# Splitting gate and up weights by casting and adding DMAs in a two-layer decoder kernel

## The chip, the cores and the metric

The kernel runs on one core of one Trainium2 chip. The metric is the device time of one execution in microseconds; a smaller time is better. TensorE multiplies matrices, VectorE and GpSimd do elementwise work, ScalarE does functions and copies, SyncE only issues DMAs. Engines run independently and wait for each other by semaphores. In profiles they are called PE (PEld for its weight loads), DVE, POOL, ACT and SP.

## The reference

Two layers over 512 tokens of width 1024, all in float32. Each layer is a half-step feed-forward block (FFN), a mixer and another half-step FFN, every one between two RMS norms. The mixer of layer 0 is attention (stick-breaking and dilated heads), that of layer 1 an mLSTM in chunks. Only the FFN matters here; its hidden width is 2816, 22 tiles of 128:

```python
def _swiglu(x, w_gate, w_up, w_down):
    return (jax.nn.silu(x @ w_gate) * (x @ w_up)) @ w_down

hf = _swiglu(_rms_norm(x, g[0]), ffn_w_gate[layer, 0], ffn_w_up[layer, 0], ffn_w_down[layer, 0])
x = x + 0.5 * _rms_norm(hf, g[1])
```

The four FFNs run in the order: layer 0 before and after attention, layer 1 before and after the mLSTM. They are called the first to the fourth FFN.

## The kernel before, in words

TensorE reads operands of the type float32r, which keeps fewer bits than float32. To come near float32, each operand is kept as two float32r tiles, a high part (the value rounded) and a low part (value minus high part), and a product is three products: high by high, high by low, low by high (`mm3`, L169). All products are recorded at L72.

A chunk of weights is 128 x 1024 float32, 512 KB: for the projections, one tile of 128 hidden columns by all 1024 inputs. `chunk` (L120) loads it into a buffer `raw` (three buffers) with a DMA from SyncE's queue (L124), casts it on ScalarE into the high part `whi` (L127) and subtracts on VectorE, or on GpSimd where `eng` says so, into the low part `wlo` (L128). There are four buffers each for `whi` and `wlo`, so a chunk's parts can be written once TensorE is done with the chunk four before. `proj` (L175) takes one chunk: 8 tiles of the contraction by three products, 24 products of 128 x 512 for all tokens.

An FFN (`ffn`, L320) begins with the first tiles in two halves of the tokens, as their norm gets ready: two tiles (four chunks) in the first and third FFN, three tiles (six chunks, four of them in a pool of their own) in the second and fourth, which follow a mixer. These first chunks come from `first_chunks` (L143). From then on `up_to(f)` (L344) runs the gate and the up chunk of tile f, one after the other:

```python
                    for n in ("gate", "up"):
                        bs.append(self.bank("pg"))
                        self.proj(bs[-1], self.chunk(a[n][l, w, f]))
```

`glu` (L394) makes h from the two: silu on ScalarE (L396), times the row scales on GpSimd (L397), times the up projection on VectorE (L398). Sixteen of the 22 tiles go through the down projection in four groups of four, by a scheme with seven products instead of eight. `right` (L443) loads two tiles of the down weights, forms sums of their blocks on GpSimd (L451, L452, L455, L457) and splits them into `dhi` and `dlo` (`wop`, by `split`, L182: cast on ScalarE at L183, subtraction on VectorE at L184); `left` (L422) does the same for h (`hop`, `hhi` and `hlo`) with VectorE alone. The seven products of a group (`products`, L464, 12 matmuls into banks `pc` per product) are put between the four chunks of the next group's first two tiles, two behind each chunk, one behind the last. So in a group TensorE has four chunks with products between, and then four without. After the last group's products follow eight chunks without any, then the down projection of the last six tiles (banks `po`), with the norm and the start of the next phase.

The order on TensorE is the order in which the program emits matmuls. The other engines' instructions, DMA issues among them, are put in each engine's queue by a scheduler when the program is built: earlier statements have precedence, but one that isn't ready, by the scheduler's own reckoning, lets later ones pass. On the chip each queue then runs in that fixed order, and an instruction that waits holds all behind it.

Of the kernel before, what the change touches and what calls it, by code (L numbers as in the profile page):

```python
# [24 lines left out]
# key block -> (bank, first column, first column in a flat row of 1280)  # L25
BLK = {0: (0, 0, 0), 1: (1, 0, 512), 3: (1, 384, 896), 2: (2, 0, 1024)}
BANKS = ((0, 512), (512, 512), (1024, 256))
# groups of four tiles of the down projection by the scheme with seven products
# [4 lines left out]
# order of the main thread's work in the mixers, and waits (ns of the tensor engine's work)  # L33
# [9 lines left out]
class Trunk:  # L43
# [25 lines left out]
    # The tensor engine's work is emitted in the order in which it should run: the main  # L69
    # thread's products, with the steps of the waiting tasks put in where they get ready.  # L70
# [11 lines left out]
    def later(self, delay, d, key, value):  # L82
        """d[key] = value once the tensor engine has worked that long"""
        def task():
            d[key] = value
            return
            yield
        self.spawn(task(), delay)

    def step(self):  # L90
        """run the task that is ready first, up to its next wait"""
        self.tasks.sort(key=lambda t: t[:2])
        _, q, gen = self.tasks.pop(0)
        self.busy = True
        d = next(gen, None)
        self.busy = False
        if d is not None:
            self.tasks.append((self.clk + d, q, gen))
# [13 lines left out]
    def exp_ln(self):  # L112
        """load the table that has both Exp and Ln"""
        self.tc.keep_in_program_order(self.nc.scalar.preload_act_table_set("natural_log_exp_and_others"))

# [4 lines left out]
    def chunk(self, src, n=1024, pool=None, tag="w", bufs=4, eng=None):  # L120
        """a chunk of weights, split into two float32r parts"""
# [10 lines left out]

    def gates(self, src):
        """the weights of the gates: high and low parts side by side, for two passes"""
# [8 lines left out]
    def first_chunks(self, ph, between=None, pool=None):  # L143
        """the first four chunks of weights of a phase, one by one beside other work"""
# [30 lines left out]
    def proj(self, out, w, t0=0, t1=T):  # L175
        """out[:, t0:t1] = (chunk of weights, K tile after K tile)^T @ xn^T"""
# [17 lines left out]
    def gain_row(self, l, i):  # L194
        """the same for the first norm, with a small load, and copied to all partitions by a product with ones"""
# [10 lines left out]
    def rstd(self, src, f=1.0, eps=EPS, sums=None):  # L206
        """1 / root of (f x the mean square of 1024 columns + eps), in two steps of 512"""
# [16 lines left out]
    def row_scales(self, fp):  # L224
        """The scheme with seven products mixes tokens, so h of a token with a small xn would be lost beside
        that of others. As h goes with the square of xn, it is divided by q = mean square / (mean square + eps),
        with 1 / q rounded to bfloat16 and at most 1e16; the norm after the FFN takes the factor back by its eps.
        1 / q of all tokens, as rows on all partitions, and that eps."""
# [18 lines left out]
    def pre(self, tb, g, wait, to=None):  # L247
        """xn^T of 128 tokens, in two parts"""
# [19 lines left out]
    def half(self, h):  # L268
        """wait for xn^T of half of the tokens"""
# [4 lines left out]
    def chain(self, tb, g, gnext, ph, out):  # L274
        """x += norm(y) for 128 tokens, and the next norm"""
# [17 lines left out]
    def down(self, hs, ws, first, then=None):  # L293
        """y[tb] (+)= h[tb] @ w for a few tiles of the contraction; then(tb) after each"""
# [17 lines left out]
    # Down projection: for the first tiles of the contraction by the scheme of Strassen and Winograd  # L312
    # on 2 x 2 blocks (halves of the tokens, pairs of tiles of the contraction, halves of the columns),
    # with seven products instead of eight:
    #   S1 = A21 + A22   S2 = S1 - A11    S3 = A11 - A21   S4 = A12 - S2
    #   T1 = B12 - B11   T2 = B22 - T1    T3 = B22 - B12   T4 = B21 - T2
    #   1: A11 B11   2: A12 B21   3: S4 B22   4: A22 T4   5: S1 T1   6: S2 T2   7: S3 T3
    #   C11 = 1 + 2   C12 = 1 + 6 + 5 + 3   C21 = 1 + 6 + 7 + 4   C22 = 1 + 6 + 7 + 5
    # The sums of products gather in PSUM, and are added to y on the way.
    def ffn(self, l, w, then, prefetch):  # L320
        nc, a = self.nc, self.a
        tc = self.tc
        with tc.tile_pool(name=f"ffn{l}{w}", bufs=1, reuse_waits="tile") as fp:
# [16 lines left out]
            with tc.tile_pool(name=f"dn{l}{w}", bufs=1, reuse_waits="tile") as dp:  # L340
                self.fp, self.dp = fp, dp
                todo = []

                def up_to(f):  # L344
                    """projections up to tile f, with products of the down projection between them"""
# [3 lines left out]
                    for n in ("gate", "up"):  # L349
                        bs.append(self.bank("pg"))  # L350
                        self.proj(bs[-1], self.chunk(a[n][l, w, f]))
# [49 lines left out]
    def hop(self, src):  # L401
        """parts of 256 columns of h"""
# [4 lines left out]
    def wop(self, src):  # L407
        """parts of 512 columns of weights"""
# [13 lines left out]
    def left(self, o, e, d):  # L422
        """operands of the products from the tiles e and d of h; the last two on the call of the result"""
# [19 lines left out]
    def right(self, o, e, d):  # L443
        """the same from two tiles of the weights"""
# [19 lines left out]
    def products(self, A, B, rest, first):  # L464
        """the seven products, in an order in which no sum waits for its reading"""
# [35 lines left out]
    def out_part(self, ws, mix, po, tb, ks):  # L501
        """a part of the second half of the contraction of an output projection, for a block of tokens"""
# [10 lines left out]
    def out_first(self, src, mix, done):  # L513
        """of that half, for two blocks of tokens, the part that doesn't need the last heads"""
# [108 lines left out]
    def qk_split(self, pq, pk):  # L623
        """q (scaled by 1/8) and k of two heads in parts, for two passes instead of three: of head r,
# [516 lines left out]
```

## Time and profile before

| | |
|---|---|
| median of three runs | 2077.33 us (2076.93 to 2078.64) |
| profiled execution, span from first to last instruction | 2074.3 us |
| own time of the profiled execution | not listed apart from the span |
| busy TensorE, VectorE, ScalarE, GpSimd | 97%, 64%, 46%, 24% |
| moved by DMA | 200.51 MB, mean 97 GB/s |

A profile gives, for each engine, what it ran and when; idle time is put down to the instruction or DMA whose semaphore came last. A group of instructions is named by its line, engine, operation and tiles (out<-in). Matmuls are pipelined, so that one of them is listed with about 390 ns although the next begins after 0.23 us; the time of many is read from the chain or from stretches. The granted clock (PEclk) is TensorE's clock as a share of its full 2.4 GHz.

### The profile page before, as it was taken

What the parts mean: (1) busy time and instruction counts of PE and PEld (TensorE: products, weight loads), DVE (VectorE), ACT (ScalarE), POOL (GpSimd) and SP (SyncE); (2) the same over time, 40 slices, a digit from 0 to 9 for tenths busy, and PEclk for the clock granted to TensorE, in tenths of its full rate; (3) what the DMA queues carried; (4) which work ended last, traced back from release to release, by engine and by line L of the source; (5) the groups of instructions that cost most, each with busy time, mean ns of one, the idle gap of its engine ahead of it and who ended that gap; (6) DMA issues with size and microseconds to landing.
All of it is one profiled execution on the core that took longest, in us unless ns stands there. A gap on an engine that the chain in (4) does not pass through costs nothing. (4 is left out here: it accounts for less than half of the span.)

```text
span 2074.3 us, 25950 instructions
## 1 busy us (share of the span) xinstructions
PE 2018.6 (97%) x9876; PEld 1677.5 (81%) x9876; DVE 1320.4 (64%) x2016; ACT 948.3 (46%) x1633; POOL 503.9 (24%) x374
## 2 busy tenths in 40 slices
PE   8999999999998999999999999999999979999998
PEld 7888887788876878888888888888888869788887
DVE  6766654656567676665487666547776786766643
ACT  5443332466775353333344333324786554443321
POOL 4322302101002342320243223021010144332111
PEclk9999999999999999999999999999999999999999
DMA  5323232232122243333223333321433222423321
GB/s 183 122 93 109 94 112 81 81 108 67 57 63 70 72 132 102 102 102 112 61 91 123 94 108 94 112 76 43 146 97 127 89 91 92 130 94 104 109 82 41
DMA packets 56119, 200.51 MB, mean 97 GB/s; under 512 B 6521, under 2 KB 6649, under 8 KB 55994
## 3 DMA queue, kind: packets, MB, share of 16 engines
q1 hardware_dynamic: 55992, 198.85, 29.8%
q8 instruction: 77, 1.26, 0.3%
q14 instruction: 48, 0.39, 0.1%
q10 hardware_dynamic: 2, 0.00, 0.0%
HBM read 196.65 MB, written 4.80 MB: 97 GB/s over the span
## 5 line engine op out<-in xcount | busy, mean ns | idle before, releaser
L72 PE MATMUL pg<-xnl,whi 128*128 128x512 f32 (+1 forms) x1568 | 584.6, 373 | 6.2 <-DVE xnl L184 6.2
L72 PE MATMUL pg<-xnh,whi 128*128 128x512 f32 (+1 forms) x1568 | 584.7, 373 | 0.1
L72 PE MATMUL pg<-xnh,wlo 128*128 128x512 f32 (+1 forms) x1568 | 583.9, 372 | 0.0
L127 ACT CAST whi<-raw 128x1024 fp32r<-128x1024 f32 x248 | 259.4, 1049 | 455.6 <-issue 202.5
L128 DVE TENSOR_TENSOR wlo<-raw,whi 128x1024 fp32r<-128x1024 f32 x227 | 289.5, 1277 | 196.2 <-ACT whi L127 192.0
L72 PEld LDWEIGHTS pg<-xnl,whi 128*128 128x128 f32 x1568 | 297.5, 190 | 61.6 <-DVE xnl L184 7.0
L72 PEld LDWEIGHTS pg<-xnh,whi 128*128 128x128 f32 x1568 | 297.5, 190 | 55.2 <-ACT xnh L183 0.5
L72 PEld LDWEIGHTS pg<-xnh,wlo 128*128 128x128 f32 x1568 | 297.5, 190 | 54.8
L397 POOL TENSOR_TENSOR h<-h,rs 128x512 f32<-128x512 f32 x88 | 143.0, 1625 | 777.3 <-ACT h L396 749.5
L184 DVE TENSOR_TENSOR dlo<-raw,dhi 128x512 fp32r<-128x512 f32 x240 | 188.3, 804 | 92.6 <-ACT dhi L183 92.0
L183 ACT CAST dhi<-raw 128x512 fp32r<-128x512 f32 x240 | 146.5, 621 | 198.1 <-DMA raw<-down 153.2
L398 DVE TENSOR_TENSOR h<-h,pg 128x512 f32<-128x512 f32 x88 | 60.0, 682 | 224.8 <-PE pg L72 221.6
L72 PE MATMUL pc<-dhi,hhi 128*128 128x512 f32 x448 | 175.2, 391 | 3.9 <-ACT hhi L183 3.9
L72 PE MATMUL pc<-dhi,hlo 128*128 128x512 f32 x448 | 175.2, 391 | 0.6 <-DVE hlo L184 0.6
L72 PE MATMUL pc<-dlo,hhi 128*128 128x512 f32 x448 | 174.8, 390 | 0.0
L482 DVE TENSOR_TENSOR y<-y,pc 128x512 f32<-128x512 f32 x192 | 128.9, 677 | 5.6 <-PE pc L72 5.4
L72 PE MATMUL pq<-xnh,whi 128*128 128x512 f32 (+1 forms) x312 | 112.8, 363 | 0.0
L72 PE MATMUL pq<-xnl,whi 128*128 128x512 f32 (+1 forms) x312 | 112.0, 359 | 0.3 <-DVE xnl L184 0.3
L72 PE MATMUL pq<-xnh,wlo 128*128 128x512 f32 (+1 forms) x312 | 111.7, 358 | 0.0
L184 DVE TENSOR_TENSOR hlo<-h,hhi 128x256 fp32r<-128x256 f32 x208 | 103.3, 514 | 8.1 <-ACT hhi L183 7.9
L183 ACT CAST hhi<-h 128x256 fp32r<-128x256 f32 x208 | 78.9, 404 | 54.9 <-DVE h L398 47.7
L72 PEld LDWEIGHTS pc<-dhi,hhi 128*128 128x128 f32 x448 | 84.2, 188 | 22.5 <-ACT hhi L183 4.8
(236 smaller groups left out, 3323.2 us busy)
## 6 DMA issues: line engine op xcount, KB each, us to landing
raw<-gate SPq DMA_DIRECT2D x88, 512.0 KB, 3.5
raw<-up SPq DMA_DIRECT2D x88, 512.0 KB, 3.5
raw<-down SPq DMA_DIRECT2D x88, 512.0 KB, 3.5
raw<-mlstm_in SPq DMA_DIRECT2D x24, 512.0 KB, 3.5
raw<-attn_in SPq DMA_DIRECT2D x16, 512.0 KB, 3.5
bt<-rows SPq DMA_DIRECT2D x8, 896.0 KB, 4.5
gb<-norm_g SPq DMA_DIRECT2D x11, 512.0 KB, 3.9
raw<-attn_v SPq DMA_DIRECT2D x8, 512.0 KB
```

The costliest lines, as they stand in the source:

```text
L72: self.nc.tensor.matmul(out, lhsT=lhsT, rhs=rhs, start=start, stop=stop, skip_group_check=True)
L127: nc.scalar.copy(hi[:, :n], raw[:, :n])
L128: sub = (eng or nc.vector).tensor_sub(lo[:, :n], raw[:, :n], hi[:, :n])
L183: self.nc.scalar.copy(hi, src)
L184: self.nc.vector.tensor_sub(lo, src, hi)
L397: self.nc.gpsimd.tensor_mul(h, h, self.rs)
L398: self.nc.vector.tensor_mul(h, h, pu)
L482: self.nc.vector.tensor_add(dst, dst, b)
```

## The change

The loop of `up_to` no longer calls `chunk`. It takes its chunks from `stream`, a new function that issues both of a chunk's parts as DMAs from GpSimd's queue: a load of the float32 weights that casts into `whi`, a copy on ScalarE that writes the negative of `whi` into `wlo`, and a second load of the same weights that is added to what `wlo` holds. Casting loads are emitted up to two chunks ahead of the one in use, adding loads one ahead. The number of buffers stays, and so do `first_chunks`, the mixers and the down projection. All else in the diff takes out comments and docstrings.

```diff
+    def stream(self, srcs, tag="w", bufs=4):
+        nc, hs, ls = self.nc, [], []
+
+        def get(i):
+            while len(hs) < min(i + 3, len(srcs)):
+                hi = self.pp.tile([P, 1024], F32R, tag=tag + "hi", bufs=bufs, name="whi")
+                lo = self.pp.tile([P, 1024], F32R, tag=tag + "lo", bufs=bufs, name="wlo")
+                nc.gpsimd.dma_start(hi, srcs[len(hs)])
+                nc.scalar.activation(lo, hi.bitcast(F32), AF.Copy, scale=-1.0)
+                hs.append((hi, lo))
+            while len(ls) < min(i + 2, len(srcs)):
+                n = len(ls)
+                nc.gpsimd.dma_start(hs[n][1], srcs[n], accum_op=ALU.add)
+                ls.append(n)
+            return hs[i]
+        return get
...
+                f0 = len(hs)
+                get = self.stream([a[n][l, w, f] for f in range(f0, NF) for n in ("gate", "up")])
...
-                    for n in ("gate", "up"):
+                    for n in range(2):
                         bs.append(self.bank("pg"))
-                        self.proj(bs[-1], self.chunk(a[n][l, w, f]))
+                        self.proj(bs[-1], get(2 * (f - f0) + n))
```

## Rows read from the trace of the kernel before

**Rows 1.** The page, busy time by engine: us, share of the span, instructions.

```profile
span 2074.3 us, 25950 instructions
PE 2018.6 (97%) x9876; PEld 1677.5 (81%) x9876; DVE 1320.4 (64%) x2016; ACT 948.3 (46%) x1633; POOL 503.9 (24%) x374
```

**Rows 2.** Table of stretches: length, busy us by engine (count), PEclk, DMA share, GB/s.

```profile
60.00:343.00 283.00, 283.00 (x1227) 230.70 (x1226) 164.07 (x246) 106.68 (x180) 71.39 (x44) 1.00 0.33 106
...
1760.00:2030.00 270.00, 267.73 (x1159) 217.71 (x1158) 163.86 (x245) 101.88 (x177) 69.05 (x44) 1.00 0.32 100
...
1208.30:1271.96 63.66, 63.66 (x277) 51.94 (x277) 40.92 (x63) 23.75 (x40) 19.39 (x12) 1.00 0.32 99
```

**Rows 3.** Chain of waits, third FFN, merged: start us, us, what.

```profile
1072.26 36.55 PE pg L72 x192
...
1114.29 5.57 PE pg L72 x24
...
1271.96 27.88 PE pg L72 x120
...
1335.63 44.61 PE pg L72 x192
```

**Rows 4.** Groups of instructions by line: busy us, mean ns, idle before, releaser.

```profile
L128 DVE TENSOR_TENSOR wlo<-raw,whi 128x1024 fp32r<-128x1024 f32 x227 | 289.5, 1277 | 196.2 <-ACT whi L127 192.0
L127 ACT CAST whi<-raw 128x1024 fp32r<-128x1024 f32 x248 | 259.4, 1049 | 455.6 <-issue 202.5 <-PE pg L72 191.3 <-DMA raw<-up 23.2
...
L128 POOL TENSOR_TENSOR wlo<-raw,whi 128x1024 fp32r<-128x1024 f32 x21 | 52.3, 2497 | 66.0 <-PE po L72 54.5 <-ACT whi L127 11.5
...
L218 POOL TENSOR_TENSOR r<-v,mhalf 128x1 f32<-128x1 f32 x48 | 30.4, 634 | 116.7 <-DVE v L215 110.5 <-DVE q L232 6.2
```

**Rows 5.** DMA issues by line: count, KB each, median us from issue to landing.

```profile
raw<-gate SPq DMA_DIRECT2D x88, 512.0 KB, 3.5
```

**Rows 6.** Timeline of ScalarE at the start of the third FFN: start us, us.

```profile
1072.11 1.06 ACT L127 CAST whi<-raw 128x1024 fp32r<-128x1024 f32 x1 [3.84 <-issue]
...
1074.54 2.19 ACT L183 CAST dhi<-raw 128x512 fp32r<-128x512 f32 x4
```

**Rows 7.** Timeline of GpSimd at the same place.

```profile
1072.34 1.29 POOL L452 TENSOR_TENSOR xa<-raw 128x512 f32<-128x512 f32 x1 [7.25 <-PE rs L242]
1073.71 2.15 POOL L457 TENSOR_TENSOR raw<-raw,xa 128x512 f32<-128x512 f32 x1
1075.83 1.62 POOL L397 TENSOR_TENSOR h<-h,rs 128x512 f32<-128x512 f32 x1
```

**Rows 8.** Table of stretches, first products of the second and fourth FFN.

```profile
737.47:752.93 15.46, 13.19 (x50) 10.02 (x49) 14.18 (x22) 9.03 (x17) 3.91 (x3) 0.89 0.43 138
1760.27:1774.16 13.89, 11.62 (x50) 8.87 (x48) 11.90 (x17) 8.41 (x17) 3.91 (x3) 1.00 0.41 123
```

**Rows 9.** Timelines of GpSimd and VectorE inside a group of the third FFN.

```profile
1180.00 1.29 POOL L451 TENSOR_TENSOR raw<-raw 128x512 f32<-128x512 f32 x1 [4.29 <-DVE dlo L184]
...
1184.90 2.28 POOL L457 TENSOR_TENSOR raw<-raw,xa 128x512 f32<-128x512 f32 x1
...
1184.42 1.60 DVE L128 TENSOR_TENSOR wlo<-raw,whi 128x1024 fp32r<-128x1024 f32 x1
```

**Rows 10.** Timeline of TensorE at the first products of the second FFN.

```profile
743.03 0.50 PE L72 MATMUL pc<-dhi,hhi 128*128 128x512 f32 x1 [1.97 <-ACT hhi L183]
...
744.07 0.50 PE L72 MATMUL pc<-dhi,hlo 128*128 128x512 f32 x1 [0.30 <-DVE hlo L184]
```

**Rows 11.** Timeline of VectorE at the same place.

```profile
740.73 1.21 DVE L128 TENSOR_TENSOR wlo<-raw,whi 128x1024 fp32r<-128x1024 f32 x1
741.87 0.68 DVE L398 TENSOR_TENSOR h<-h,pg 128x512 f32<-128x512 f32 x1
742.47 1.21 DVE L128 TENSOR_TENSOR wlo<-raw,whi 128x1024 fp32r<-128x1024 f32 x1
```

## The prediction

> **What bounds the kernel now.** The first view is the page: TensorE is busy for 2018.6 of 2074.3 us, so 55.7 us of the span are all that any change off TensorE can win [rows 1]. The second is the table of stretches. Between the first projections of an FFN and its last products, where the change works, TensorE is busy 283.00 of 283.00 us in the first FFN and 267.73 of 270.00 us in the last, while VectorE has over a third of the time free [rows 2]. The one idle piece there, 2.27 us, comes once in each of the two FFNs that follow a mixer; I come to it below. The rest of the 55.7 us lies at the changes of phase, around norms, where no chunk of the changed loop is split. The third view is the chain of waits. In an FFN it is TensorE alone: 24 products of one chunk take 5.57 us, eight chunks without work between them 44.61 us [rows 3].
>
> So the 200 us of VectorE that this change frees are nearly all hidden already, and its result hangs on two things: whether each chunk's parts still arrive before TensorE wants them, and whether that 2.27 us goes.
>
> **What is removed, term by term.** The changed loop has 40 chunks in the first and third FFN (20 tiles, two chunks each) and 38 in the two others, 156 in all. For each, VectorE loses a subtraction of mean 1277 ns, 199 us together; SyncE loses an issue; ScalarE's cast of 1049 ns becomes a copy with a factor of -1 of the same 128x1024, which I price alike [rows 4]. Cover: TensorE in [rows 2]. Worth on the path: 0, but for the relief below.
>
> **What is added.** GpSimd issues 312 DMAs. No row has one, so I bound the issue from below by 0 beyond what a landing of 3.5 us from SyncE's queue contains [rows 5], from above by GpSimd's dearest operation on a whole chunk, 2.5 us, and take 0.6, what its smallest operation costs (128x1, 634 ns) [rows 4]; it is nearest to an instruction that touches no chunk. In a group of 63.66 us (eight chunks, seven products) GpSimd is busy 19.39 us [rows 2], so 16 issues would fill it only from 2.77 us each.
>
> The DMA engines: in that group they carry 12 loads of 512 KB in 0.32 of the time, 1.70 us each [rows 2]. Afterwards it is four loads for the down projection, eight casting and eight adding ones. At 1.70 us that is 34 of 63.66 us. The 16 fit as long as they take under (63.66 - 6.8) / 16 = 3.55 us each.
>
> **The latency of a chunk** is what matters. Four buffers serve each part, so a buffer is free when TensorE has finished the chunk four before; then load, negation and adding load run one after the other. Inside a run of chunks there are 3 x 5.57 = 16.7 us for it [rows 3]. At the start of the first and third FFN there is less: the first four chunks are worked on in two halves, buffer 0 is free at 1072.11 us, when ScalarE's cast takes it [rows 6], and TensorE starts the first chunk of the changed loop at 1072.26 + 36.55 - 27.88 = 1080.93 us [rows 3]: 8.8 us. Before, cast and subtraction filled 2.6 of these, the raw data being there already; the new load can't be made before the buffer is free. The chain there:
>
> - In GpSimd's queue: three of its operations stand at that place, 1.29, 2.15 and 1.62 us [rows 7]. Low 0, high 5.1; I take the first, 1.3.
> - Casting load: low 3.5, a plain load [rows 5]; high 3.5 + 2.5; taken 3.5 + 0.6 = 4.1.
> - Negation: 1.05, after a wait for ScalarE of 0 to 2.2 (four casts in a row stand there [rows 6]); taken 1.05 + 0.5.
> - Adding load: low 3.5; high two loads in series (it reads the tile and writes it) and the dear issue, 9.5; taken one transfer more than a plain load, 3.5 + 1.7 + 0.6 = 5.8, since the two reads should overlap.
>
> Taken 12.75 us, low 8.05, high 23.85. Against 8.8 us TensorE waits 3.9 us at the start, low 0, high 15. The second chunk has its buffer 2.9 us later and is wanted 5.57 us later, so it asks for nothing more. A stall costs more than its length: in the FFNs after the mixers 2.27 us of idle cost 15.46 and 13.89 us where a pair of products and a chunk take 5.45 + 5.57 = 11.02, so 4.4 and 2.9; in the first of them the granted clock fell to 0.89 behind the wait [rows 8]. I add 1.0 for that. Two starts: 2 x (3.9 + 1.0) = **9.8 us lost**, low 0, high 32. In the other two FFNs six chunks are worked on first, 12 halves, and two buffers are free early: 0.
>
> The Trainium skill, "DMA: Bandwidth & Descriptors", section "Latency and other measured facts", has a first byte after about 1 us from GpSimd's queue and 0.6 us from SyncE's. By that, an estimate, each of the two loads would pay 0.4 us in place of my 0.6, and the loss would be 9.0 us. No run here shows it yet.
>
> Inside the runs: 12.75 against 16.7, covered, 4 us to spare; what lies in front in GpSimd's queue there are its four subtractions of a group (1.3 to 2.3 us each [rows 9]), apart by other waits. High: 23.85 - 16.7 = 7.1 us for every four chunks in a row, some five times an FFN, 142 us in all.
>
> **The relief.** After a mixer, a first product waits 1.97 us for a ScalarE cast and 0.30 us for VectorE [rows 10]. On VectorE the tile h that is cast waits in line behind a chunk's subtraction at 740.73 us, and the low part of h behind another at 742.47 [rows 11]. Without them h comes 1.14 us (740.73 to 741.87) and its low part another 1.1 us sooner. In front of these stand parts of the down weights, which GpSimd's subtractions feed; they stay. Taken: 1.14 + 0.3 of idle and as much again at what a wait costs on top, 1.7 us each, **3.4 us won**. High: both losses whole, 7.3. Low: the wait grows by two issues of 0.6 in front of GpSimd's subtractions, 2.4 us lost.
>
> **Sum.** 2074.3 + 9.8 - 3.4 = 2080.7 us of span. The page gives no time of its own for the profiled execution besides the span; the median of the runs, 2077.33, is 3.0 us above it, and I carry that over: **2083.7 us**.
>
> **Rivals.** *The starts are covered too, and the relief is all there is.* For it: the low ends are plain loads, and only 0.75 us of the low sum isn't needed. Against: two loads and a negation in a row without a wait is the best case. 2074.3 - 7.3 to 2074.3 - 3.4, plus 3.0: 2070 to 2074.
>
> *Nothing shows.* Path and relief cancel, with a path near 10.5 us: 2 x (1.7 + 0.5) - 3.4 + 2077.3 = 2078. For it: both terms are small. If the casting load rounded nothing at all, the same instructions would run and the time would be the same, so that case hides here.
>
> *The path outlasts the runs too.* It decides from 16.7 us on. Price at 18: starts 2 x (9.2 + 1.0) = 20, inside 1.3 + 1.0 for each of five places in four FFNs = 46, relief 3.4: 2140. For it: GpSimd and ScalarE work in order, and a load or negation that is late holds what stands behind it (GpSimd's product with the row scales, ScalarE's casts of h and of the down weights). Against: 5 us of margin.
>
> *The DMA engines become the bound*, from 3.55 us a load on. At 4 us a group takes 4 x 1.7 + 64 = 70.8 us, 7.1 more, over 156 / 8 = 19.5 groups 139 us: 2216. Against: 0.32 of share now.
>
> A further way it could be lost: VectorE may hold GpSimd up while it writes what a DMA needs. A row shows the two sharing something: a subtraction of GpSimd takes 1.29 us alone and 2.28 us beside a chunk's subtraction on VectorE [rows 9]. If each issue waited for one VectorE operation of 1.2 us, the path would be 15.2 us and the time 2088.6; that lies within the forecast's own range. The Trainium skill, "SBUF — State Buffer", section "Who interferes with whom", says that only VectorE's two-port modes lock GpSimd out, and that an operation on two tensors takes the read side alone; by that this loss would be nil. The row agrees that reads collide; it has no write of descriptors.
>
> **How the numbers follow.** 0.2%, 4.2 us, is about what a measurement of this kernel tells from no change. Forecast (path 10.5 to 16.7 us): 0.45, 2078 to 2096 (the end without relief), of it 0.12 within 4.2 us and 0.33 slower. Starts covered: 0.22, 0.18 faster and 0.04 within. Nothing shows: 0.16, all within. Path outlasts the runs: 0.12; DMA engines bound: 0.05, both slower. Faster 0.18, same 0.32, slower 0.50. The range goes from 2071, the relief nearly whole, to 2130, short of the last two rivals' prices, which leaves out some 0.16. The forecast's own range, 2078 to 2096, stands beside it.
>
> **What would show it.** Right: a gap of 2 to 8 us in TensorE before the first 128x512 chunk of the first and third FFN, ended by a GpSimd DMA; none inside the runs; VectorE's busy time about 1120 us; the first products after the mixers waiting less. Wrong: gaps in every run (path), a DMA share near 1 in a group (engines), or ScalarE idle for long before its negations. A time under 2073 would say that the loads were made earlier than I believe, one over 2100 that GpSimd's queue or its loads are dearer.

## The result and the profile after

The changed kernel takes 2204.06 us, median of four runs (2200.42 to 2212.44), beside 2077.13 us for the kernel before (2074.28 to 2078.64): a ratio of 1.0615, interval 1.0591 to 1.0639. The forecast was 2083.7 with a range to 2130. The direction was right, the size far off: 127 us instead of 6.

The page of the changed kernel, its first rows, answers to [rows 1]:

```profile
span 2198.4 us, 26036 instructions
PE 2059.8 (94%) x9876; PEld 1694.6 (77%) x9876; DVE 1153.7 (52%) x1860; ACT 934.2 (42%) x1633; POOL 677.5 (31%) x686
```

VectorE lost its work, as it should, and no engine has much. Of the 124.1 us that the span grew by, TensorE stands idle for 82.9 more (138.6 against 55.7) and is busy for 41.2 more with the same products. With the second part goes its granted clock, whose mean over the execution fell from 0.988 to 0.971.

TensorE's waits, longest groups (us in total, times, longest), show where it stands idle:

```profile
PE pg L72 <- DMA wlo<-gate: 37.6, 17, 3.8
PE pc L72 <- DVE y L504: 20.5, 11, 2.7
...
PE pc L72 <- ACT hhi L203: 18.1, 10, 2.4
PE pg L72 <- DMA whi<-gate: 6.6, 2, 3.9
...
PE pc L72 <- ACT y L502: 4.0, 2, 2.4
...
PE pg L72 <- DMA wlo<-up: 1.7, 2, 1.5
```

Only 45.9 us are waits for the new loads. Another 42.6 are waits of the down projection's products (`pc`) for ScalarE and VectorE; before, 4.5 us of such waits stood in the whole kernel (in [rows 10], one of its two places). So something spreads from the gate and up chunks to work that has nothing to do with them.

The table of stretches, from the first products of the second group of the first FFN to those of the third and of the fourth, answers to the whole group in [rows 2] (us, TensorE, its weight loads, VectorE, ScalarE, GpSimd, granted clock, DMA share, GB/s):

```profile
142.40:213.81 71.41, 66.20 (x277) 52.80 (x276) 33.06 (x55) 22.52 (x40) 28.07 (x29) 0.98 0.61 147
213.81:285.10 71.29, 66.09 (x277) 52.74 (x276) 33.14 (x55) 22.53 (x40) 28.16 (x30) 0.98 0.61 148
```

The same 277 products took 63.66 us. The four FFNs grew by 28, 31, 32 and 31 us, the mixers by next to nothing. In the first and third FFN the stretch from the first group's products to the second's still takes 63.7 us and the two after it 71.3 to 71.4; in the second and fourth all three together are 19.5 and 18.9 us longer. These twelve stretches hold 69 us of the loss, the starts some 31, the ends of the FFNs nearly all of the rest. In the first stretch above TensorE is idle for 5.2 us more and busy for 2.5 more. With the second part goes the clock, 0.98 in the mean against 1.00: behind a wait of 2.45 us at 173.38 six products in a row come 0.43 us apart instead of 0.23, at the lower of the two levels.

DMA issues (count, KB each, median us to landing) answer to [rows 5], and the groups of GpSimd and ScalarE that the change added to [rows 4] (busy us, mean ns, idle time before, releasers):

```profile
raw<-down SPq DMA_DIRECT2D x88, 512.0 KB, 6.4
whi<-gate POOLq DMA_DIRECT2D x78, 512.0 KB, 6.4
whi<-up POOLq DMA_DIRECT2D x78, 512.0 KB, 5.8
wlo<-gate POOLq DMA_DIRECT2D x78, 512.0 KB, 5.5
wlo<-up POOLq DMA_DIRECT2D x78, 512.0 KB, 5.5
```

```profile
L148 POOL DMA_DIRECT2D wlo<-gate x78 | 69.3, 888 | 408.3 <-ACT hhi L203 205.1 <-ACT wlo L144 168.5 <-PE pc L72 22.8
L148 POOL DMA_DIRECT2D wlo<-up x78 | 67.8, 869 | 338.1 <-ACT wlo L144 313.3 <-ACT dhi L203 8.5 <-ACT h L418 8.1
...
L144 ACT ACTIVATE wlo<-whi 128x1024 fp32r<-128x1024 f32 x156 | 165.0, 1059 | 642.1 <-DMA whi<-gate 416.1 <-DMA whi<-up 109.8 <-issue 105.7
```

Two engines wait in their queues: ScalarE 526 us for casting loads ahead of its negations, GpSimd 746 us ahead of its adding loads, most of it for those negations. (Where a cast of h is named, it is the instruction of ScalarE behind the negation; the adding load starts 0.3 us after the negation's end there too, as at 147.83.) GpSimd's timeline through the first stretch above, of its DMA issues alone (four subtractions stand from 160.57 to 166.69 and again from 182.04 to 188.28), says what that means:

```profile
147.83 0.88 POOL L148 DMA_DIRECT2D wlo<-gate  x1 [4.89 <-ACT hhi L203]
150.94 0.88 POOL L148 DMA_DIRECT2D wlo<-up  x1 [2.23 <-ACT wlo L144]
151.50 0.89 POOL L143 DMA_DIRECT2D whi<-gate  x1
...
159.54 0.87 POOL L148 DMA_DIRECT2D wlo<-gate  x1 [5.96 <-ACT wlo L144]
...
166.64 0.60 POOL L143 DMA_DIRECT2D whi<-up  x1
171.80 0.86 POOL L148 DMA_DIRECT2D wlo<-up  x1 [4.56 <-ACT wlo L144]
172.36 0.86 POOL L143 DMA_DIRECT2D whi<-gate  x1
...
181.41 0.87 POOL L148 DMA_DIRECT2D wlo<-gate  x1 [7.00 <-ACT wlo L144]
...
193.61 0.85 POOL L148 DMA_DIRECT2D wlo<-up  x1 [4.79 <-ACT wlo L144]
194.16 0.86 POOL L143 DMA_DIRECT2D whi<-gate  x1
...
202.91 0.88 POOL L148 DMA_DIRECT2D wlo<-gate  x1 [6.67 <-ACT hhi L203]
...
211.28 0.86 POOL L148 DMA_DIRECT2D wlo<-up  x1 [6.91 <-ACT wlo L144]
...
212.97 0.87 POOL L143 DMA_DIRECT2D whi<-gate  x1
...
223.08 0.90 POOL L143 DMA_DIRECT2D whi<-gate  x1
```

Between 142.40 and 213.81 GpSimd waits 43.0 us ahead of eight adding loads and is busy for 28.1: together 71.1 of 71.4 us. It waits for no free buffer and for nothing of TensorE's. A lap of its queue (gate's casting load, wait for landing and negation, gate's adding load, its own subtractions, up's casting load, the same wait again, up's adding load) takes 20.9, 21.8, 18.8 and 10.1 us from 151.50 to 223.08, 71.58 for the four of a group. That is TensorE's group. GpSimd is 31% busy on the page and has no free time in these groups.

The order in this queue is not that of the diff. There, the casting load of the next chunk is emitted ahead of a chunk's adding load, so that two round trips would overlap. The scheduler put six of the eight adding loads of this group directly behind their own casting loads, with nothing between but GpSimd's other work; only at 147.83 and 150.94 stand both casting loads of a pair in front. And the round trips are longer than with casting loads alone: a casting load lands in 6.4 and 5.8 us beside the adding loads, in 3.8 in the run without them, told of below.

### The profile page after: what moved, and what is told of

It reads as the page before. It is cut to its first block, busy times and chain, and to the rows that moved or that the text cites. A ratio compares the mean times of both kernels' runs of the same rounds, so it can differ in the third digit from the quotient of the medians.

```text
span 2198.4 us, 26036 instructions
## 1 busy us (share of the span) xinstructions
PE 2059.8 (94%) x9876; PEld 1694.6 (77%) x9876; DVE 1153.7 (52%) x1860; ACT 934.2 (42%) x1633; POOL 677.5 (31%) x686
## 5 line engine op out<-in xcount | busy, mean ns | idle before, releaser
L72 PE MATMUL pg<-xnh,wlo 128*128 128x512 f32 (+1 forms) x1568 | 594.1, 379 | 39.4 <-DMA wlo<-gate 37.6
L72 PE MATMUL pg<-xnh,whi 128*128 128x512 f32 (+1 forms) x1568 | 594.0, 379 | 6.9 <-DMA whi<-gate 6.6
L72 PE MATMUL pg<-xnl,whi 128*128 128x512 f32 (+1 forms) x1568 | 592.2, 378 | 5.9 <-DVE xnl L204 5.9
L144 ACT ACTIVATE wlo<-whi 128x1024 fp32r<-128x1024 f32 x156 | 165.0, 1059 | 642.1 <-DMA whi<-gate 416.1
L72 PEld LDWEIGHTS pg<-xnh,whi 128*128 128x128 f32 x1568 | 303.4, 194 | 64.2 <-issue 7.4
L204 DVE TENSOR_TENSOR dlo<-raw,dhi 128x512 fp32r<-128x512 f32 x240 | 219.8, 930 | 220.7 <-ACT dhi L203 220.7
L72 PE MATMUL pc<-dhi,hhi 128*128 128x512 f32 x448 | 179.9, 402 | 42.7 <-DVE y L504 20.5
L148 POOL DMA_DIRECT2D wlo<-gate x78 | 69.3, 888 | 408.3 <-ACT hhi L203 205.1
L148 POOL DMA_DIRECT2D wlo<-up x78 | 67.8, 869 | 338.1 <-ACT wlo L144 313.3
L203 ACT CAST dhi<-raw 128x512 fp32r<-128x512 f32 x240 | 141.3, 615 | 24.4 <-DMA raw<-down 19.3
L419 POOL TENSOR_TENSOR h<-h,rs 128x512 f32<-128x512 f32 x88 | 119.0, 1352 | 82.3 <-ACT h L418 53.8
L127 ACT CAST whi<-raw 128x1024 fp32r<-128x1024 f32 x92 | 95.6, 1047 | 50.4 <-issue 24.0
```

The lines of the kernel that those rows point to most:

```text
L72: self.nc.tensor.matmul(out, lhsT=lhsT, rhs=rhs, start=start, stop=stop, skip_group_check=True)
L127: nc.scalar.copy(hi[:, :n], raw[:, :n])
L144: nc.scalar.activation(lo, hi.bitcast(F32), AF.Copy, scale=-1.0)
L148: nc.gpsimd.dma_start(hs[n][1], srcs[n], accum_op=ALU.add)
L203: self.nc.scalar.copy(hi, src)
L204: self.nc.vector.tensor_sub(lo, src, hi)
```

## The experiments

Three theories stood at the beginning: **A**, ScalarE's queue is held by negations that wait for casting loads; **B**, the row of slot, load, negation and adding load outlasts the four buffers; **C**, the DMA engines or the writing of descriptors are the bound. **D**, GpSimd's lap, came after the first four runs, and the timeline above was read then. Every time below is a median; ratios are to the kernel before on the same chip.

**The second load a casting one too, no negation**

```diff
-                nc.scalar.activation(lo, hi.bitcast(F32), AF.Copy, scale=-1.0)
...
-                nc.gpsimd.dma_start(hs[n][1], srcs[n], accum_op=ALU.add)
+                nc.gpsimd.dma_start(hs[n][1], srcs[n])
```

> ScalarE's negation is left out and the second load is a plain casting load like the first, so the low part is not computed; the count of GpSimd's loads (312) and the traffic stay. Theory A (ScalarE's queue is held by negations that wait for casting loads, 526 us of idle time): the hold is gone, 2080 to 2100 us. Theory B (slot, load, negation, adding load in a row outlast the four buffers): the row is shorter by two steps, 2080 to 2100 as well, with the starts of the runs still costing some 4 us each. Theory C (the DMA engines or GpSimd's descriptor writing are the bound): 2170 to 2210, as both are unchanged.

2081.01 us, ratio 1.0022 (1.0012 to 1.0031). The count of loads and their bytes are unchanged, so C falls as far as it means these. What the kernel leaves out is the low part. GpSimd's casting loads now wait for TensorE, whose pace it is, four laps being 63.67 us in its timeline:

```profile
134.79 0.53 POOL L143 DMA_DIRECT2D whi<-gate  x1 [4.52 <-PE pg L72]
...
156.83 0.53 POOL L143 DMA_DIRECT2D whi<-gate  x1 [7.19 <-PE pg L72]
...
176.15 0.53 POOL L143 DMA_DIRECT2D whi<-gate  x1 [5.69 <-PE pg L72]
...
187.30 0.53 POOL L143 DMA_DIRECT2D whi<-gate  x1 [4.52 <-PE pg L72]
...
198.46 0.53 POOL L143 DMA_DIRECT2D whi<-gate  x1 [4.52 <-PE pg L72]
```

**No adding load**

```diff
-                nc.gpsimd.dma_start(hs[n][1], srcs[n], accum_op=ALU.add)
```

> The adding load is left out, so the low part is only the negated high part; the casting load and the negation that waits for it stay in their places, and 156 of 312 of GpSimd's loads are gone. Theory A: ScalarE's queue is held as before, 2150 to 2200 us. Theory B: 5.5 us of the row of 16 are gone, which puts it inside the cover of the four buffers, 2090 to 2120. Theory C: half of the added traffic is gone, 2080 to 2110, with plain loads back from 6.4 us to about 4.

2074.66 us, ratio 0.9987 (0.9973 to 1.0000). A was wrong here, and the bands of B and C lay too high: ScalarE still waits for casting loads, and it costs nothing. In its waits (us in total, times, longest):

```profile
ACT wlo L144 <- DMA whi<-gate: 133.7, 64, 4.6
...
ACT wlo L144 <- DMA whi<-up: 122.1, 72, 3.5
```

What is missing is an instruction on GpSimd that waits for the negation.

**The negation on GpSimd, and on VectorE**

```diff
-                nc.scalar.activation(lo, hi.bitcast(F32), AF.Copy, scale=-1.0)
+                nc.gpsimd.tensor_scalar(lo, hi.bitcast(F32), -1.0, None, op0=ALU.mult)
```

> The negation is done on GpSimd, ahead of the adding load that it already issues; ScalarE waits for no casting load any more. Theory A with ScalarE as the holder: 2100 to 2150 us, as GpSimd's wait of 482 us for the negation only changes its name. Theory B: the row gets no shorter (the negation takes 1.3 to 2.5 us there instead of 1.05 plus 0.5), 2200 to 2230. Theory C: 2190 to 2210.

2494.09 us, ratio 1.2021 (1.1989 to 1.2053): no theory on record held. GpSimd now does in its own queue what it only waited for; four laps take 86.4 us (casting loads of gate at 145.65 and, four later, at 232.03). With `nc.vector` in the same place:

> The negation is done on VectorE; ScalarE waits for no casting load any more, VectorE does. Theory A: the hold moves to the engine that empties TensorE's banks, so it costs the same or more, 2190 to 2260 us, with VectorE's idle time on casting loads near the 526 us that ScalarE had. Theory B: the row is as long as it was, 2195 to 2210. Theory C: 2195 to 2210. A result under 2150 speaks against A in any form in which the engine doesn't matter.

2283.74 us, ratio 1.0991 (1.0966 to 1.1016), above the bands of all three. Four laps take 72.9 us, little more than with ScalarE. Much of the rest lies in VectorE's queue: VectorE waits some 485 us for casting loads ahead of its negations, and TensorE's waits for the sums of products that VectorE makes (`y`) rise from 20.5 to 69.0 us.

**The order on GpSimd's queue**

```diff
-            while len(hs) < min(i + 3, len(srcs)):
+            while len(hs) < min(i // 2 * 2 + 4, len(srcs)):
...
-            while len(ls) < min(i + 2, len(srcs)):
+            while len(ls) < min((i + 1) // 2 * 2 + 2, len(srcs)):
...
-                nc.gpsimd.dma_start(hs[n][1], srcs[n], accum_op=ALU.add)
+                self.tc.keep_in_program_order(nc.gpsimd.dma_start(hs[n][1], srcs[n], accum_op=ALU.add))
```

> The same loads, negations and buffers as the changed kernel; only the order on GpSimd's queue is another: both casting loads of a gate and up pair come ahead of the pair's adding loads, so that GpSimd waits for one round trip of load and negation a pair instead of two. Theory D, formed after the first four runs (GpSimd's queue is the bound: it works in order, waits out load and negation twice a pair, and has four subtractions of 6.2 us besides; its lap was 20.9 and 21.8 us in the changed kernel, between the casting loads at 151.50, 172.36 and 194.16, where two casting loads without a negation gave TensorE's 19.3): a lap of some 17 to 19 us, so 2080 to 2130 us. Theory A (ScalarE's waits are what counts): its negations still wait for their loads, 2170 to 2205. Theory B (the row of slot, load, negation and adding load outlasts the four buffers): the gate's adding load comes later than before, 2200 to 2260.

2125.95 us, ratio 1.0222 (1.0200 to 1.0244). D, and D alone, had this. (The scheduler also moved some of the down projection's first products on TensorE in the second and fourth FFN: they begin 1.9 us behind the first chunk of the changed loop, not 16.7; in the first and third they stay behind the chunks. The order of the diff, held as it is written, was not run.) The expectation's comparison with a single lap of 19.3 us was careless: TensorE's laps are 22.0, 19.3, 11.2 and 11.2, and it is the four together that count. They take 64.7 us here, and a group 64.5. GpSimd's waits ahead of the gate's adding loads fall from 408.3 to 151.5 us; the one at 164.65 waits for nothing any more:

```profile
149.38 0.91 POOL L143 DMA_DIRECT2D whi<-gate  x1
...
164.07 0.59 POOL L143 DMA_DIRECT2D whi<-up  x1
164.65 0.93 POOL L148 DMA_DIRECT2D wlo<-gate  x1
...
169.74 0.89 POOL L148 DMA_DIRECT2D wlo<-up  x1 [4.15 <-ACT wlo L144]
170.28 0.91 POOL L143 DMA_DIRECT2D whi<-gate  x1
```

ScalarE's waits stay, and cost nothing:

```profile
ACT wlo L144 <- DMA whi<-gate: 412.9, 72, 8.2
ACT wlo L144 <- DMA whi<-up: 99.2, 35, 6.5
```

That is 512 us against 526 in the changed kernel, with 78 us less time.

**The four subtractions of the down weights on VectorE**

```diff
     def right(self, o, e, d):
-        g = self.nc.gpsimd
+        g = self.nc.vector
```

> The four subtractions of each pair of down tiles go from GpSimd to VectorE; loads, negations and adding loads stay. Theory D: GpSimd's lap loses up to 6.2 us in the places that have them (21.8 to about 15.6, under TensorE's 19.3), 2090 to 2130 us. Theory A: ScalarE still waits for casting loads, 2180 to 2210. Theory B: nothing of the row itself changes, 2190 to 2210. VectorE's busy time rises by some 60 to 130 us in each.

2117.43 us, ratio 1.0193 (1.0169 to 1.0217). Nothing of the loads changed, only what stands in GpSimd's queue beside them; its four laps fall to 64.9 us (149.75 to 214.68).

**A fifth buffer**

```diff
-            while len(hs) < min(i + 3, len(srcs)):
+            while len(hs) < min(i + 4, len(srcs)):
...
-            while len(ls) < min(i + 2, len(srcs)):
+            while len(ls) < min(i + 3, len(srcs)):
```

(every fifth chunk in two tiles of the pool of the down weights; `raw` with two buffers).

> A fifth buffer for the high and low parts, with both loads started one chunk earlier (for the room, the raw tiles of the down projection have two buffers instead of three). Theory B: a fifth slot gives the row 8.3 us more cover, 2080 to 2120 us. Theory D: GpSimd's lap has the same waits and the same work, 2180 to 2205. Theory A: 2180 to 2205.

2218.43 us, ratio 1.0673 (1.0654 to 1.0692), slower than the changed kernel, four laps 73.1 us. D's band ended at 2205. More cover does not help a queue that is full, so B falls. How much of the 14 us on top of the changed kernel's time comes from the two `raw` buffers or the other order wasn't tried.

**The adding load alone**

```diff
-                nc.gpsimd.dma_start(hi, srcs[len(hs)])
+                raw = self.pp.tile([P, 1024], F32, tag="raw", bufs=3, name="raw")
+                nc.sync.dma_start(raw, srcs[len(hs)])
+                nc.scalar.copy(hi, raw)
```

> The high part is rounded by ScalarE from a plain load of SyncE, as in the kernel before; ScalarE then negates it and GpSimd's adding load makes the low part. So the adding load alone of the two new loads is used, and 156 loads are on each queue. Theory D: GpSimd waits only for a negation whose input was loaded ahead by SyncE, 2070 to 2095 us. Theory A: ScalarE waits less, as plain loads land early, 2080 to 2110. Theory B: the row ends with the adding load's 5.5 us but begins ahead, 2080 to 2110. If the adding load's time on the DMA engines (about 3.0 us of all 16 each, against 1.7 of a casting load, from the queue's share of 33.3% here and 25.3% with two casting loads) is itself the cost, 2130 or more.

2114.47 us, ratio 1.0173 (1.0152 to 1.0194): over the bands of all three theories and under that of the DMA engines. Not the runs are the cost, whose laps are TensorE's 63.7 us, but four starts, one in each FFN:

```profile
PE pg L72 <- DMA wlo<-gate: 32.9, 4, 8.9
```

**The starts split as before**, in the changed kernel and in the one with the other order:

```diff
             while len(hs) < min(i + 3, len(srcs)):
+                if len(hs) < 4:
+                    hs.append(self.chunk(srcs[len(hs)]))
+                    continue
...
                 n = len(ls)
+                if n < 4:
+                    ls.append(n)
+                    continue
```

> The changed kernel, but in each of the four FFNs the first four chunks of the run are split as before (SyncE's load, ScalarE's rounding, VectorE's subtraction), so no start of a run waits for the long row. Theory D: only the starts are taken back, which cost 8.8, 6.4, 9.3 and 6.4 us in the trace of the changed kernel (31 in all, of which up to 7 of relief after the mixers may be lost again); GpSimd's lap in the rest of the runs stays over TensorE's, 2170 to 2185 us. The forecast as written (the starts are the cost, inside the runs four buffers cover the row): 2080 to 2095.

2206.18 us, ratio 1.0624 (1.0600 to 1.0647): nothing gained, and both expectations missed. The first products come at 74.5 us instead of 78.8, but the group from them to the next takes 69.0 us instead of 63.7. The likely reading: in the changed kernel the stall at the start let GpSimd get ahead; without it, it falls behind within the next group. Where GpSimd sets the pace a start has no cost of its own.

> Both together: GpSimd's casting loads ahead of the adding loads of a pair, and the first four chunks of a run split as before. Theory D: the run with the other order alone gave 2126, of which the starts are some 30 to 40 us; 2083 to 2097. If what was left over in that run came from the DMA engines' traffic (the loads of down land in 5.7 us there instead of 3.5): 2110 to 2126.

2111.48 us, ratio 1.0166 (1.0148 to 1.0184): 14.5 us less than without it, not 30, and in the band that was named for the DMA engines' traffic. The stretches between groups still take 64.8 to 65.6 us in the first FFN up to 67.8 in the third and up to 73.9 in the fourth. Which of the two it is was open here; the run with all three edits, below, decides it.

**The casting load alone**

```diff
-                nc.scalar.activation(lo, hi.bitcast(F32), AF.Copy, scale=-1.0)
+                raw = self.pp.tile([P, 1024], F32, tag="raw", bufs=3, name="raw")
+                nc.sync.dma_start(raw, srcs[len(hs)])
+                nc.vector.tensor_sub(lo, raw, hi.bitcast(F32))
...
-                nc.gpsimd.dma_start(hs[n][1], srcs[n], accum_op=ALU.add)
```

> The high part by GpSimd's casting load, a plain load of the same chunk by SyncE, and VectorE's subtraction for the low part; no negation and no adding load. Theory D: nothing on GpSimd's queue waits for ScalarE, 2073 to 2085 us, though the traffic is that of two loads a chunk. If two loads a chunk cost by themselves: 2100 or more.

2079.65 us, ratio 1.0009 (1.0000 to 1.0018). Casting loads cost next to nothing.

**Both edits and the subtractions on VectorE; the adding load alone with the old starts.** No new code: the first is the order, the starts and the subtractions of above together.

> All three of the edits that took time off GpSimd's queue or the starts: casting loads ahead of the pair's adding loads, the first four chunks of a run split as before, and the four subtractions on VectorE. Theory D: GpSimd's four laps of a group fall to TensorE's 63.7 us (they summed to 71.6 in the changed kernel, 64.7 with the other order alone, 64.9 with the subtractions on VectorE alone) and no start waits, so 2078 to 2092 us. If what was left in the run with the first two of these edits (2111) is the DMA engines' traffic or ScalarE's waits for casting loads: 2105 or more.

2072.95 us, ratio 0.9975 (0.9965 to 0.9984), under D's band too. The whole loss is gone, and 5 us more (the last experiment says whose they are). 280 of the 312 new loads are still there, half of them adding ones, with their negations. So the rest of the loss was GpSimd's queue too, and neither the traffic nor ScalarE's waits.

> SyncE's plain load, ScalarE's rounding and negation, GpSimd's adding load, with the first four chunks of each run split as before. The run without that last edit gave 2114 us with GpSimd's laps at TensorE's 63.7 a group, and its loss was four starts of 9.9, 11.5, 9.8 and 10.7 us. Theory D: without them 2072 to 2086 us, so the adding load costs nothing inside the runs though it takes about 3 us of all 16 DMA engines. If the starts only move the wait into the runs, as they did in the changed kernel: 2105 to 2116.

2081.13 us, ratio 1.0016 (1.0006 to 1.0026). In runs that GpSimd doesn't pace, the starts were a cost of their own, 33 us, and the adding loads inside the runs cost next to nothing.

**The relief, tried in the kernel before**: GpSimd makes the low parts of a run's first two chunks after a mixer, and then of its first four (`f0 + 2`).

```diff
-                        self.proj(bs[-1], self.chunk(a[n][l, w, f]))
+                        self.proj(bs[-1], self.chunk(a[n][l, w, f], sub=self.nc.gpsimd if w and f < f0 + 1 else None))
```

> The kernel before, but in the second and fourth FFN, which follow a mixer, the low parts of the run's first two chunks are made by GpSimd's subtraction instead of VectorE's. In the changed kernel and in the one without adding loads the first products of these FFNs came 2.9 to 3.9 and 2.2 to 2.9 us earlier against their surroundings, as VectorE had nothing of the run's in front of the splits of h. If that relief is VectorE's queue: 2.5 to 6 us less than before, a ratio of 0.9970 to 0.9988. If GpSimd's slower subtraction (2.5 us) makes the chunk late instead: no change or up to 4 us more.

2078.79 us, ratio 1.0002 (0.9993 to 1.0011). The edit missed its target: by the trace the subtractions beside h in [rows 11] belong to the next two chunks. TensorE waited 1.97 and 0.30 us, as in [rows 10].

> As the earlier try at the relief, but for the first four chunks of the run in the second and fourth FFN, not the first two: in that try VectorE still had two subtractions of chunks around the tile h (744.18 and 745.91 us in its trace), and TensorE's first product waited the same 1.97 and 0.30 us. If the relief is VectorE's queue alone: both waits go, 2.5 to 6 us less, 2071 to 2075. If the down weights that GpSimd's subtractions feed are as late as h: no change, 2077 to 2080.

2083.58 us, ratio 1.0024 (1.0013 to 1.0035), slower than either expectation. TensorE's one long wait at the first products of the second FFN doubled:

```profile
747.76 0.80 PE L72 MATMUL pc<-dhi,hhi 128*128 128x512 f32 x1 [4.25 <-ACT hhi L183]
```

In GpSimd's timeline its subtraction of a chunk, 2.40 us at 736.38, stands ahead of the product that makes h, which starts at 741.70. The hold moved from VectorE's queue to GpSimd's.

**The subtractions of the down weights on VectorE, in the kernel before**: the diff of above on `before`.

> The kernel before, with nothing but the four subtractions of each pair of down tiles on VectorE instead of GpSimd (0.68 us there in place of 1.3 to 1.8). It tells what in the one version that was faster than the kernel before (2072.95 us, ratio 0.9975) came from this edit. If that gain is the tiles of down coming earlier to the first products after the mixers, this kernel has it too: 2070 to 2074 us. If it needs VectorE free of the chunks' subtractions, as the relief of the forecast says: 2076 to 2082, VectorE having some 75% of its time filled inside the FFNs.

2072.92 us, ratio 0.9979 (0.9970 to 0.9987): the same gain as the best version of the change, without the change. The groups of two of the four subtractions, on GpSimd in the kernel before and on VectorE here, and the stretch from before the first products of the second FFN on (columns as above):

```profile
L457 POOL TENSOR_TENSOR raw<-raw,xa 128x512 f32<-128x512 f32 x32 | 62.3, 1948 | 2.2 <-DVE dlo L184 2.1
L455 POOL TENSOR_TENSOR raw<-raw 128x512 f32<-128x512 f32 x32 | 53.6, 1677 | 0.2
```

```profile
L457 DVE TENSOR_TENSOR raw<-raw,xa 128x512 f32<-128x512 f32 x32 | 22.0, 687 | 0.4
L455 DVE TENSOR_TENSOR raw<-raw 128x512 f32<-128x512 f32 x32 | 21.9, 684 | 0.0
```

```profile
736.50:751.00 14.50, 14.50 (x65) 11.83 (x64) 13.56 (x25) 8.63 (x17) 1.82 (x1) 1.00 0.49 150
```

A subtraction takes 0.68 us in place of 1.95 and 1.68 (in the two other lines 1.39 and 1.36), and TensorE, with its first products at 741.04 us, waits for nothing in the stretch, though VectorE still has every chunk's subtraction and is busy for 13.56 of 14.50 us. The Trainium skill, "GPSIMD Engine Reference", section "Engine selection", puts elementwise operations on VectorE, GpSimd being about twice as slow with two inputs; the trace agrees, at 2.0 to 2.8 times over the four lines.

## Why the prediction was wrong

**TensorE bounds the kernel, and VectorE's relief is worth nothing inside the runs**: right. Without adding loads, VectorE's 200 us gone, the time moved by 0.13%.

**Durations**: right for each load by itself. A casting load was taken at 4.1 us to land, and the one into `whi` lands in 3.8 to 3.9 in the runs with two casting loads and without adding loads, but in 6.4 (gate) and 5.8 (up) in the changed kernel, beside adding loads; the working had no term for that. The adding load was taken at 5.8 and lands in 5.5 in the median. The issue was taken at 0.6: 0.53 to 0.59 where only casting loads are issued, 0.87 to 0.89 for an adding one. The Trainium skill ("DMA: Bandwidth & Descriptors", "Latency and other measured facts") has the first byte 0.4 us later from GpSimd's queue than from SyncE's; the traces agree, with 3.8 to 3.9 us to landing against a plain load's 3.5.

**What is added, GpSimd's queue**: this is the step that failed. It held that 16 issues would fill GpSimd only from 2.77 us each and priced them at 0.6. The price left out that an adding load can't be issued before the negation, so that GpSimd stands in front of it, with all its work behind. That wait is 746 us over 156 loads, 4.8 us each on average and 43.0 us in a group of eight. With it, 28 us of GpSimd's busy time and 43 of waiting make 71, and no such group fits in 63.66. The working had the numbers: the casting load's 4.1 us, of which 0.6 is its issue, and the negation's 1.55 make 5.05 us of wait for an adding load right behind its own casting load. Eight of them are 40 us a group, on top of the 19.39 in [rows 2] and of 16 issues of 0.6: 69 against 63.66. It did not have the order. By the order of the diff two round trips overlap; with half the wait, an estimate from the same numbers, the sum is 49 and fits. So the step needed a term for the waits in either order, and by this estimate only the order that the scheduler made, seen in the trace after, makes the sum too large.

**Inside the runs, 12.75 against 16.7 us, covered**: wrong for the same reason. It compared the delay of one chunk with the time that four buffers give, which says whether one chunk can be on time, not how many GpSimd can serve in a given time. A fifth buffer left the time above the changed kernel's; the same loads, negations and buffers in another order, in which GpSimd has both casting loads of a pair under way before it waits, took 78 us off. The same passage put four subtractions of GpSimd in a group; [rows 2] has twelve operations there, eight of them subtractions.

**The starts**: 4.9 us in the first and third FFN, 0 in the others, had been forecast. In the trace the first products, counted from the first chunk of the changed loop, come later by 8.8, 6.4, 9.3 and 6.4 us. In the first FFN TensorE waits twice, 2.66 us at 46.15 for a high part and 3.83 at 50.67 for the low part of the first chunk (between 20 and 90 us, in total, times, longest):

```profile
PE pg L72 <- DMA wlo<-gate: 3.8, 1, 3.8
PE pg L72 <- DMA whi<-gate: 2.7, 1, 2.7
```

That is 6.5 us against 3.9. (TensorE's order is not quite the program's here: the scheduler put the first products with the high parts of three chunks ahead of the first one with a low part.) The first chunk's casting load is issued at 33.47, when its buffer is free, its negation begins at 39.82, its adding load is issued at 42.77: 17.2 us to 50.67, where the working took 12.75. In the second FFN the first two chunks are early, as forecast, but the third, which needs a buffer of the chunks before, takes 17.6 us from its issue at 747.14 and makes TensorE wait 3.36. So the size of the latency was wrong as well, both loads landing later than taken. Yet the starts were no cost of their own in this kernel (taking them back gained nothing), and one where the runs had air (33 us for four).

**The relief**: 3.4 us forecast for the two FFNs together, 7.3 at most. The stretch from the first products to the second ones, which answers to [rows 8]:

```profile
772.72:783.75 11.03, 11.03 (x50) 9.04 (x49) 7.43 (x15) 5.58 (x12) 2.64 (x3) 1.00 0.99 224
1858.19:1869.20 11.01, 11.01 (x49) 9.03 (x48) 7.25 (x15) 5.58 (x12) 2.65 (x3) 1.00 0.96 225
```

15.46 and 13.89 us have become 11.03 and 11.01, with no wait: 4.4 and 2.9, the stated upper end. Some of that is luck, as the stalls at the start gave h and the down weights 6.4 us more. The run without adding loads has no such stalls; there the stretches from the first to the second group are 3.5 and 2.2 us shorter than before. That freeing VectorE is enough is not shown: with two casting loads it has none of these chunks' subtractions either, but ScalarE waits 8.76 us for down weights until 738.80, and the second FFN's first products still wait (in total, times, longest):

```profile
PE pc L72 <- ACT hhi L203: 2.8, 1, 2.8
```

That the down weights from GpSimd "stay" in front was too strict: making those sooner removes the same waits with VectorE as full as ever.

**The rivals**: the nearest was the path that outlasts the runs, at 0.12 and 2140 us. Its argument, GpSimd and ScalarE work in order and hold what stands behind, was the mechanism; its price was for a chunk that is late now and then, not for a queue that is full. ScalarE's half of it didn't matter: 512 us of its waits cost under 50 us of time in one run, 256 nothing in another. That the DMA engines become the bound didn't happen: their share in the slow groups is 0.61. The sign for a time over 2100, GpSimd's queue or its loads dearer than believed, named the right place. (Its own range, 2078 to 2096, ends at 2095 by its sum.) VectorE's busy time was forecast at about 1120 us and is 1153.7; subtractions of the down weights take 930 ns in the mean where they took 804.

## What to carry to other kernels

An instruction that waits at the head of a queue fills that queue as work does: before a step is moved to an engine, add up busy time and waits for one turn of its loop and compare the sum with the bound engine's turn, whatever the busy share says. Take the order of the queue from a trace of the changed program where a scheduler makes it, not from the source. If a pair of dependent DMAs has to go through one queue, issue the first of several ahead of the second of any, and take other work off that queue. And when a changed kernel wins, give the kernel before the same helper edits: here one of them held the whole gain.

## What the runs showed of the hardware

An adding load keeps the DMA engines busy far longer than a casting one of the same 512 KB. By the queue's share of the span over its loads (q0 on the pages of the run with the adding load alone, 156 loads in a span of 2113.3 us, and of the run with two casting loads, 312 in 2082.5):

```profile
q0 software_dynamic: 22464, 81.80, 23.1%
```

```profile
q0 software_dynamic: 44928, 163.60, 25.3%
```

The first is 3.13 us of all 16 engines for a load, the second 1.69, about what a plain load takes ([rows 2], 1.70). And loads that share the engines with adding loads land later, plain ones of SyncE too: 6.4 us for the down weights in the changed kernel, 4.6 in the run with the adding load alone, 3.9 with two casting loads, 3.5 in the run without adding loads.
